# A first mixer in float32r parts: its input projections as three products each, and the first shift's modulation made by TensorE between them

## The chip, the cores and the metric

The kernel runs on one core of a Trainium2 chip. The metric is device time in microseconds (us), the median over several runs; smaller is better. The profile comes from one further execution, whose own time stands beside it.

## The reference

Two decoder layers over 256 tokens of width 1024. What matters here is the start of the first one:

```
c_act = silu(c)
mod = c_act @ ada_w[layer] + ada_b[layer]        # 1024 -> 6 * 1024
sh_m, sc_m, g_m, sh_f, sc_f, g_f = split(mod, 6)
h = rmsnorm(x, norm_mix_w) * (1 + sc_m) + sh_m
p = h @ e_w_in                                   # 1024 -> 1536: u (512), v (512), pool part (512)
ya = mixer_a(p[:, :1024])                        # gelu; layernorm of v; causal W_s in chunks of 128; u * sv
yb = mixer_b(p[:, 1024:])                        # trailing means minus the token, a 128x128 product per group
x = x + g_m * (concat(ya, yb) @ e_w_out)
```

A dense SwiGLU follows in layer 0; layer 1 has a convolution and latent attention, then a top-2-of-8 expert SwiGLU with 352 MB of weights. All inputs are float32.

## The kernel before

**Weights.** Every weight comes from HBM in chunks of 128 x 2048 float32 (1 MB) into a ring of five buffers (`raw`, line 98). The list `order` gives the sequence of the loads, all on SyncE's queue; a load is issued when the buffer five places earlier has been read for the last time. In the first stretch the sequence is, for each of four quarters q of the inner dimension: the scale's modulation chunk `("ada", 0, 1, q)`, the shift's `("ada", 0, 0, q)`, and the weight chunk `("vp", q)`; then `("u", 0)`, four chunks of the gate's modulation `("ada", 0, 2, q)` with `("u", 1)` among them, and the output projection's `("eo", c)`.

**Float32 products, and products in parts.** Most of the kernel multiplies in float32r parts: ScalarE casts a chunk to float32r (`H`, line 121, two halves), VectorE subtracts that from the chunk (`L`, line 124, two halves), the activations are split alike (lines 301 and 306, or `store_hl`), and TensorE adds H·H, L·H and H·L (`mm3_b`, lines 316, 318 and 322; `mm3_a`, lines 334, 335 and 337). Two places use plain float32 products: the v and pool columns of the first projection (line 649, a 128x512 product of each half weight with each half of the tokens) and its u columns (`gate_u`, line 666). Their operand `h0` is one float32 tile, `hF`.

**Modulation.** `ada` makes 256 of the modulation's values with two VectorE instructions of 128x1024 (line 568: multiply by silu(c), sum along the row) and an addition of the bias (line 596). `ada_rows` does the same on TensorE from weights stored by input rows: 8 products with the chunk (line 579), a copy of the result by ScalarE (line 585); the function `turn` that it gives back then turns the row into columns by two small products (line 589) and adds the bias on VectorE (line 591). Before the change `ada_rows` serves the second norm's scale and shift alone, in their last two quarters.

**Norm and transposes.** `HT.flip` transposes the normed tokens on TensorE (line 285); `HT.evac` multiplies by the scale and adds the shift from PSUM (line 299; the scale's column from line 207) and, where it splits, casts to `H` (line 301); `HT.low` makes `L` (line 306).

**Order of the work.** Between `tc.manual_schedule` and `hand.close()` the engines take their instructions as the code is written. After `hand.close()` a scheduler sets the order up to the next such stretch, in the middle of the output projection. Every engine works through its own list in order. After the vp products come `gate_u(0)`, the pooling products (lines 704 to 706, 713), `gate_u(1)`, the layernorm of v (statistics on VectorE, lines 683 to 687; the rest on GpSimd, lines 688 to 691), the product of v with `wsT` (line 730), `yaT` (lines 737 and 739), and the output projection with its residual (lines 365 and 366).

Of the kernel before, what the change touches and what calls it, by code (L numbers as in the profile page):

```python
# [17 lines left out]
D = 1024  # L18
S = 256
KD = 8  # L20
# [4 lines left out]
CH = 2048  # L25
RING = 5
RING2, RING3 = 8, 3
HB, LB = 6, 5
# [15 lines left out]
def trunk_kernel(ctx, tc, x_in, c_in, pos_in, cols_in, rows_in,  # L44
# [3 lines left out]
    vec, act, pe, gp, sp = nc.vector, nc.scalar, nc.tensor, nc.gpsimd, nc.sync  # L48
# [77 lines left out]
    def high_part(raw, f):  # L126
        h = Halves("H", HB, f)
        for q in range(2):
            h.copy(q, raw)
        return h  # L130
# [20 lines left out]
    def psa(n="pa"):  # L151
        return psA.tile([128, 512], F32, tag="A", name=nm(n))
# [16 lines left out]
    for i in range(2):  # L169
        t = per.tile([128, D], F32, name=f"x{i}")  # L170
# [137 lines left out]
    def mm3_b(outs, ks, xH, xL, wH, wL, first, last, by_tile=False):  # L308


        tiles = list(enumerate(outs))
        for group in ([[t] for t in tiles] if by_tile else [tiles]):
            for m, k in enumerate(ks):
                for i, os_ in group:
                    for n, o in enumerate(os_):
                        pe.matmul(o, xH(k, i), wH(k, n), start=first and m == 0, stop=False)  # L316
                    for n, o in enumerate(os_):
                        pe.matmul(o, xL(k, i), wH(k, n), start=False, stop=False)  # L318
            for m, k in enumerate(ks):
                for i, os_ in group:  # L320
                    for n, o in enumerate(os_):
                        pe.matmul(o, xH(k, i), wL(k, n), start=False, stop=last and m == len(ks) - 1)  # L322

    def toks(t):
        return lambda k, i: t[:, k, i * 128:(i + 1) * 128]

    def wcols(w, k0, kw, bounds):

        return lambda k, n: w[:, (k - k0) * kw + bounds[n][0]:(k - k0) * kw + bounds[n][1]]

    def mm3_a(o, wH, wL, hH, hL):

        for k in range(KD):
            pe.matmul(o, wH(k), hH[:, k, :], start=(k == 0), stop=False)  # L334
            pe.matmul(o, wH(k), hL[:, k, :], start=False, stop=False)  # L335
        for k in range(KD):
            pe.matmul(o, wL(k), hH[:, k, :], start=False, stop=(k == KD - 1))  # L337
# [210 lines left out]
    def raw_of(*key):  # L548
        fetch(place[key] + RING)
        return raws.pop(key)  # L550

    def split_of(*key):
        return split_raw(*raw_of(*key))

    def ada(l, p, q):

        half, end = ada_steps(l, p, q)
        half(0)
        half(1)
        end()  # L560
# [11 lines left out]
    def ada_rows(l, p, q, *before):  # L572

        raw, _ = raw_of("ada", l, p, q)
        ps = psb()
        for kk in range(2):
            for g in range(4):
                k = g * 2 + kk
                pe.matmul(ps[g * 32:(g + 1) * 32, 0:256], ccol[:, k:k + 1].to_broadcast([128, 32]),
                          raw[:, k * 256:(k + 1) * 256], start=(kk == 0), stop=(kk == 1), skip_group_check=True)  # L580
        j = p * 8 + q * 2
        for f in before:
            f()
        row = adp.tile([128, 512], F32, tag="junk", name=nm("row"))[:, 0:256]
        act.copy(row, ps[:, 0:256])

        def turn():
            for a in range(2):
                pe.matmul(ps[:, 256 + a:257 + a], row[:, a * 128:(a + 1) * 128], quart, start=True, stop=True)
            lo = K_AB + l * 48 + j  # L590
            vec.tensor_tensor(mods[:, l, j:j + 2], ps[:, 256:258], cols[:, lo:lo + 2], OP.add)
        return turn
# [4 lines left out]

    BD = [(0, 512), (512, 1024)]

    with Phase("mix0", w8=5, w4=5, w2=6) as pool:  # L600
        sm = pool
        lrow = pool.tile([128, 2048], F32, tag="w8", name="lrow")
        bands = pool.tile([128, 4, 3, 128], F32, tag="w8", name="bands")
# [27 lines left out]
        hand = ctx.enter_context(ExitStack())  # L631
        hand.enter_context(tc.manual_schedule(engines=MAN | {mybir.EngineType.Pool}))
        xn = normed()
        ht = HT(pool, xn, 0, False, split_it=False)
        h0 = ht.full
        vp = [[psa() for _ in range(2)] for _ in range(2)]
        ht.flip(0)
        for q in range(4):
            if q < 3:
                ht.flip(q + 1)  # L640
            ada(0, 1, q)
            ada(0, 0, q)
            ht.evac(q)
            w, _ = raw_of("vp", q)
            for kk in range(2):
                k = q * 2 + kk
                for part in range(2):
                    for i in range(2):
                        pe.matmul(vp[part][i], h0[:, k, i * 128:(i + 1) * 128],  # L649
                                  w[:, kk * D + part * 512:kk * D + (part + 1) * 512], start=(k == 0), stop=(k == 7))  # L650
            if q == 1:
                mean_bands()
        hand.close()
# [4 lines left out]
        uT = pool.tile([128, 4, S], F32, tag="w4", name="uT")  # L658

        def gate_u(c):  # L660
            w, _ = raw_of("u", c)
            ps = psb()
            for cc in range(2):
                for k in range(KD):
                    o = k * 256 + cc * 128
                    pe.matmul(ps[:, cc * 256:(cc + 1) * 256], w[:, o:o + 128], h0[:, k, :], start=(k == 0), stop=(k == 7))
            return ps

        gu_ps = gate_u(0)
# [1165 lines left out]
```

## Time and profile before

| | |
|---|---|
| median of 3 runs | 1250.69 us (1250.29 to 1253.85) |
| profiled execution: time, span | 1250.61 us, 1248.6 us |
| TensorE busy | 1199.2 us, 96% of the span |
| ScalarE, VectorE, GpSimd busy | 501.3, 735.3, 67.7 us |
| moved by DMA | 468.11 MB, mean 375 GB/s |
| granted TensorE clock, mean | 0.989 |

The profile's rows give the start and the length of an instruction or of a group in microseconds from the start of the span; PE is TensorE, PEld its weight loads, ACT ScalarE, DVE VectorE, POOL GpSimd, SP SyncE. A float32 product stands as two products in the trace (x16 for 8 instructions of line 649), a float32r product as one. In groups of pipelined products the spacing (length over count) is what one costs; the mean length of a single one includes its tail.

### The profile page before, as it was taken

The numbers are of one execution on the slowest core, as the hardware profiler recorded it, in microseconds if no ns is written. First come the engines' busy times: TensorE is split into PE (matmuls) and PEld (weight loads), VectorE is DVE, ScalarE is ACT, GpSimd is POOL, SyncE is SP. The second block draws the span as 40 slices with busy tenths as digits, with TensorE's granted clock in tenths as the row PEclk, the third lists the DMA queues.
The fourth block names the chain that finished last, engine by engine and source line by source line (L and its number), as shares of the span: only waits on it lengthen the run. The fifth ranks groups of instructions, "written<-read, shape, count | busy, mean of one in ns | idle before, by whom it ended". The sixth has DMA issues, their size and how long they took to land.

```text
span 1248.6 us, 18665 instructions
## 1 busy us (share of the span) xinstructions
PE 1199.2 (96%) x7255; PEld 866.1 (69%) x7255; DVE 735.3 (59%) x1098; ACT 501.3 (40%) x775; POOL 67.7 (5%) x105
## 2 busy tenths in 40 slices
PE   5999999999999899999999999999999999999997
PEld 2577999997987666666666676666675666666663
DVE  5797988886895355546264656263555652653531
ACT  2147443445763234444153344252433541433410
POOL 2810000001320000000000000000000000000000
PEclk9999999999999799999999999999999999999999
DMA  9898999984657899999999999999999999999995
GB/s 357 352 376 306 354 337 349 355 313 176 237 203 277 343 405 421 419 419 419 419 420 419 419 420 419 420 419 420 419 419 412 418 419 420 420 420 418 420 418 202
DMA packets 65904, 468.11 MB, mean 375 GB/s; under 512 B 7568, under 2 KB 7824, under 8 KB 9616
## 3 DMA queue, kind: packets, MB, share of 16 engines
q1 hardware_dynamic: 65520, 466.32, 92.5%
q8 instruction: 59, 0.97, 0.3%
q10 hardware_dynamic: 288, 0.52, 0.1%
q14 instruction: 37, 0.30, 0.1%
HBM read 465.76 MB, written 1.05 MB: 374 GB/s over the span
## 4 chain that ended last, share of the span: by engine, by line
PE 85%; DVE 7%; issue 2%; ACT 2%; POOL 1%; DMA 1%; SPq 0%; DVEq 0%; ACTq 0%; POOLq 0%
PE gu L1527 20%; PE o L1547 10%; PE o L316 3%; PE g L316 3%; PE pb L337 3%; PE g L318 3%; PE u L318 3%; PE o L318 3%; PE u L316 3%; PE o L322 3%; PE g L322 3%; PE pb L335 3%; PE u L322 3%; PE pb L334 3%; PE pa L649 2%
## 5 line engine op out<-in xcount | busy, mean ns | idle before, releaser
L121 ACT CAST H<-raw 128x1024 fp32r<-128x1024 f32 x350 | 344.2, 1047 | 34.2 <-PE pb L335 13.2
L147 DVE TENSOR_TENSOR raw<-raw,H 128x1024 fp32r<-128x1024 f32 x252 | 297.5, 1222 | 39.9 <-ACT H L121 22.6
L1527 PE MATMUL gu<-raw,hgS 128*64 128x256 f32 x2240 | 253.8, 383 | 0.0
L1527 PEld LDWEIGHTS gu<-raw,hgS 128*64 128x64 f32 x2240 | 157.4, 137 | 89.0 <-issue 13.8
L124 DVE TENSOR_TENSOR L<-raw,H 128x1024 fp32r<-128x1024 f32 (+1 forms) x98 | 118.2, 1219 | 26.6 <-PE pb L337 14.5
L1547 PE MATMUL o<-raw,aS 128*64 128x512 f32 x560 | 130.4, 599 | 0.0
L568 DVE SCALAR_TENSOR_TENSOR junk<-raw,cact 128x1024 bf16<-128x1024 f32 x88 | 108.8, 1259 | 8.4 <-DMA raw<-in_ada 8.2
L334 PE MATMUL pb<-hH,H 128*128 128x256 f32 x432 | 103.1, 279 | 0.0
L335 PE MATMUL pb<-hL,H 128*128 128x256 f32 x432 | 102.9, 279 | 0.0
L1533 DVE TENSOR_TENSOR msg<-msg,gu 128x256 f32<-128x256 f32 x35 | 14.7, 421 | 125.2 <-ACT msg L1532 125.1
L1547 PEld LDWEIGHTS o<-raw,aS 128*64 128x64 f32 x560 | 37.0, 137 | 64.3 <-issue 60.0
L334 PEld LDWEIGHTS pb<-hH,H 128*128 128x128 f32 x432 | 81.2, 188 | 0.4
L335 PEld LDWEIGHTS pb<-hL,H 128*128 128x128 f32 x432 | 81.1, 188 | 0.4
L1481 DVE TENSOR_TENSOR msg<-msg,u 128x512 f32<-128x512 f32 x21 | 14.4, 687 | 109.0 <-ACT msg L1480 109.0
L1532 ACT ACTIVATE msg<-gu 128x256 f32<-128x256 f32 x35 | 13.4, 384 | 161.3 <-PE gu L1527 161.2
L1480 ACT ACTIVATE msg<-g 128x512 f32<-128x512 f32 x21 | 12.5, 597 | 151.3 <-PE g L322 151.3
L316 PE MATMUL g<-H,hgH 128*128 128x512 f32 x168 | 67.3, 401 | 0.0
L322 PE MATMUL u<-raw,hgH 128*128 128x512 f32 x168 | 66.5, 396 | 0.0
L318 PE MATMUL g<-H,hgL 128*128 128x512 f32 x168 | 66.5, 396 | 0.0
L318 PE MATMUL u<-H,hgL 128*128 128x512 f32 x168 | 66.4, 395 | 0.0
L316 PE MATMUL u<-H,hgH 128*128 128x512 f32 x168 | 66.3, 395 | 0.0
L322 PE MATMUL g<-raw,hgH 128*128 128x512 f32 x168 | 66.3, 394 | 0.0
(391 smaller groups left out, 1631.4 us busy)
## 6 DMA issues: line engine op xcount, KB each, us to landing
raw<-in_mgu SPq DMA_DIRECT2D x224, 1024.0 KB, 16.0
raw<-in_mdn SPq DMA_DIRECT2D x112, 1024.0 KB, 15.3
raw<-in_ada SPq DMA_DIRECT2D x48, 1024.0 KB, 6.9
raw<-in_fgu SPq DMA_DIRECT2D x22, 1024.0 KB, 7.7
raw<-in_fdn SPq DMA_DIRECT2D x11, 1024.0 KB, 7.5
raw<-in_oin_c SPq DMA_DIRECT2D x6, 1024.0 KB, 5.3
raw<-in_ein_vp SPq DMA_DIRECT2D x4, 1024.0 KB, 9.3
raw<-in_eout SPq DMA_DIRECT2D x4, 1024.0 KB, 7.2
```

The lines of the kernel that those rows point to most:

```text
L121: act.copy(self.to(q), raw[:, q * self.f:(q + 1) * self.f])
L124: eng.tensor_tensor(self.to(q), raw[:, q * self.f:(q + 1) * self.f], high.half(q).bitcast(F32), OP.subtract)
L147: vec.tensor_tensor(l[:, at], raw[:, at], h.half(q).bitcast(F32), OP.subtract)
L316: pe.matmul(o, xH(k, i), wH(k, n), start=first and m == 0, stop=False)
L318: pe.matmul(o, xL(k, i), wH(k, n), start=False, stop=False)
L322: pe.matmul(o, xH(k, i), wL(k, n), start=False, stop=last and m == len(ks) - 1)
L334: pe.matmul(o, wH(k), hH[:, k, :], start=(k == 0), stop=False)
L335: pe.matmul(o, wH(k), hL[:, k, :], start=False, stop=False)
L337: pe.matmul(o, wL(k), hH[:, k, :], start=False, stop=(k == KD - 1))
L568: vec.scalar_tensor_tensor(junk, raw[:, a * D:(a + 1) * D], 1.0, cact, OP.mult, OP.mult, accum_out=mods[:, l, j + a:j + a + 1])
L1527: pe.matmul(gu[HALF[h], n * 256:(n + 1) * 256], g_.full[:, k, :], w[:, lo:lo + 256], start=(k == 0 and n == 0), stop=(k == KD - 1), skip_g ...
L1547: pe.matmul(o[HALF[h]], a[:, kk, c, :], w[:, kk * D + h * 512:kk * D + (h + 1) * 512], start=(j == 0 and c == 0 and kk == 0), stop=(j == 6 ...
```

## The change

The vp and u products of the first mixer become three products of float32r parts. `HT` now splits its result (`hH`, `hL` instead of `hF`). Each vp chunk is cast and subtracted in halves, and its 8 float32 products become 24 float32r products of the same size in two calls of `vp_part`, one for each 128 rows of the quarter; each u chunk is split too, and its 16 float32 products of 128x256 become 48. The shift's chunks `("ada", 0, 0, q)` leave VectorE: they are stored by input rows and go through `ada_rows`, the products with chunk q + 1 between the two calls of `vp_part` of quarter q, and `turn` at the head of quarter q + 1. One more 8 KB buffer is given to the phase. The sequence of the loads is as before.

```diff
         xn = normed()
-        ht = HT(pool, xn, 0, False, split_it=False)
-        h0 = ht.full
+        ht = HT(pool, xn, 0, False)
+        h0H, h0L = ht.H, ht.L
         vp = [[psa() for _ in range(2)] for _ in range(2)]
+
+        def vp_part(q, ks, w):
+            mm3_b([[vp[part][i] for part in range(2)] for i in range(2)], ks, toks(h0H), toks(h0L),
+                  wcols(w[0], q * 2, D, BD), wcols(w[1], q * 2, D, BD), ks[0] == 0, ks[-1] == KD - 1)
+
         ht.flip(0)
+        ada(0, 1, 0)
+        turn = ada_rows(0, 0, 0)
         for q in range(4):
+            turn()
+            ht.evac(q)
+            raw, _ = raw_of("vp", q)
+            w = high_part(raw, CH), Halves("L", LB, CH)
+            ht.low(q, vec)
+            for half in range(2):
+                w[1].less(half, raw, w[0])
             if q < 3:
                 ht.flip(q + 1)
-            ada(0, 1, q)
-            ada(0, 0, q)
-            ht.evac(q)
-            w, _ = raw_of("vp", q)
-            for kk in range(2):
-                k = q * 2 + kk
-                for part in range(2):
-                    for i in range(2):
-                        pe.matmul(vp[part][i], h0[:, k, i * 128:(i + 1) * 128],
-                                  w[:, kk * D + part * 512:kk * D + (part + 1) * 512], start=(k == 0), stop=(k == 7))
+                ada(0, 1, q + 1)
+            vp_part(q, (q * 2,), w)
+            if q < 3:
+                turn = ada_rows(0, 0, q + 1)
+            vp_part(q, (q * 2 + 1,), w)
             if q == 1:
                 mean_bands()
         hand.close()
...
         def gate_u(c):
-            w, _ = raw_of("u", c)
+            w = split_of("u", c)
             ps = psb()
             for cc in range(2):
-                for k in range(KD):
-                    o = k * 256 + cc * 128
-                    pe.matmul(ps[:, cc * 256:(cc + 1) * 256], w[:, o:o + 128], h0[:, k, :], start=(k == 0), stop=(k == 7))
+                mm3_a(ps[:, cc * 256:(cc + 1) * 256], *(lambda k, t=t: t[:, k * 256 + cc * 128:k * 256 + cc * 128 + 128] for t in w),
+                      h0H, h0L)
             return ps
```

TensorE's list, before, from the end of the vp quarter 0 into quarter 1 (`pt` is the transposes' PSUM tile, `pa` the four sums of vp, `raw` the weight chunk, `hF` the activations):

```order
L649 MATMUL pa_156<-raw_172,hF_153 128x512
L649 MATMUL pa_157<-raw_172,hF_153 128x512
L285 MATMUL pt_204<-ident,xn_137 128x128 x2
L285 MATMUL pt_204<-ident,xn_138 128x128 x2
L649 MATMUL pa_154<-raw_183,hF_153 128x512
L649 MATMUL pa_155<-raw_183,hF_153 128x512
```

Between two quarters TensorE has only the transposes of the quarter after next. The same place now (`pb_238` holds the shift's row of quarter 1 and, after line 589, its columns; `H_272` is the first half of the vp chunk of quarter 1):

```order
L322 MATMUL pa_155<-L_210,hH_153 128x512
L322 MATMUL pa_157<-L_210,hH_153 128x512
L322 MATMUL pa_156<-L_210,hH_153 128x512
L322 MATMUL pa_158<-L_210,hH_153 128x512
L589 MATMUL pb_238<-quart,row_247 128x1 x2
L285 MATMUL pt_281<-ident,xn_137 128x128 x2
L285 MATMUL pt_281<-ident,xn_138 128x128 x2
L316 MATMUL pa_155<-H_272,hH_153 128x512
L316 MATMUL pa_157<-H_272,hH_153 128x512
```

The turning products of quarter 1's shift now stand behind the last product of quarter 0. ScalarE's list, before, after the norm (`v` and `pp` are vp's results):

```order
L261 ACTIVATE xn_137<-x_92,ss_135 128x1024
L261 ACTIVATE xn_138<-x_94,ss_136 128x1024
L673 ACT_TABLE_LOAD
L673 ACTIVATE v_367<-pa_154 128x512
L673 ACTIVATE v_369<-pa_155 128x512
```

The same list now, from quarter 0 into quarter 1 (`hf` is what `evac` wrote):

```order
L301 CAST hH_153<-hf_197 128x512
L121 CAST H_203<-raw_168 128x1024
L121 CAST H_205<-raw_168 128x1024
L585 COPY row_247<-pb_238 128x256
L301 CAST hH_153<-hf_266 128x512
L121 CAST H_272<-raw_179 128x1024
L121 CAST H_274<-raw_179 128x1024
```

ScalarE had nothing to do between norm and results; now a quarter's weight casts stand behind the cast of its activations. VectorE's list, before, from the last `evac` on (`bn`, `mv`, `lrs` are the layernorm's statistics):

```order
L299 TENSOR_SCALAR hF_153<-pt_265,acol_315,mods 128x256 x2
L683 BN_STATS bn_376<-v_367 128x6
L683 BN_STATS bn_386<-v_369 128x6
L685 BN_AGGR mv_378<-bn_376 128x2
L685 BN_AGGR mv_388<-bn_386 128x2
L687 TENSOR_SCALAR lrs_380<-mv_378 128x1
L687 TENSOR_SCALAR lrs_390<-mv_388 128x1
```

The same stretch now, from the last half of vp's low part on (`raw_369` is the first u chunk, 405 and 439 are chunks of the gate's modulation):

```order
L124 TENSOR_TENSOR L_448<-raw_307,H_443 128x1024
L568 SCALAR_TENSOR_TENSOR junk_481,mods<-raw_405,cact 128x1024
L568 SCALAR_TENSOR_TENSOR junk_483,mods<-raw_405,cact 128x1024
L124 TENSOR_TENSOR L_499<-raw_369,H_495 128x1024
L596 TENSOR_TENSOR mods<-mods,cols 128x2
L568 SCALAR_TENSOR_TENSOR junk_488,mods<-raw_439,cact 128x1024
L568 SCALAR_TENSOR_TENSOR junk_490,mods<-raw_439,cact 128x1024
L124 TENSOR_TENSOR L_501<-raw_369,H_497 128x1024
L596 TENSOR_TENSOR mods<-mods,cols 128x2
L691 BN_STATS bn_561<-v_552 128x6
L691 BN_STATS bn_571<-v_554 128x6
L693 BN_AGGR mv_563<-bn_561 128x2
```

The scheduler put four modulation instructions and both low halves of the first u chunk ahead of the layernorm's statistics.

## Rows read from the trace of the kernel before

**Rows 1.** The page's first line.

```profile
span 1248.6 us, 18665 instructions
```

**Rows 2.** Windows: stretch, length, each engine's busy time (instructions), clock, DMA share, GB/s.

```profile
17.00:52.00 35.00, 32.19 (x74) 14.46 (x75) 22.14 (x47) 1.98 (x4) 20.31 (x28) 1.00 0.97 388
52.00:71.00 19.00, 19.00 (x104) 16.87 (x103) 15.55 (x23) 5.99 (x12) 14.47 (x8) 1.00 0.81 320
71.00:82.00 11.00, 11.00 (x57) 9.14 (x57) 10.93 (x16) 8.28 (x11) 0.00 (x0) 1.00 0.91 359
115.00:260.00 145.00, 145.00 (x1055) 136.35 (x1054) 128.80 (x217) 66.46 (x92) 0.00 (x0) 1.00 0.92 343
500.00:1240.00 740.00, 729.66 (x4275) 479.40 (x4276) 367.45 (x417) 279.55 (x369) 0.00 (x0) 1.00 1.00 413
```

**Rows 3.** Timeline of TensorE, the vp products: start, length, idle before.

```profile
17.04 9.94 PE L649 MATMUL pa<-raw,hF 128*128 128x512 f32 x16 [3.49 <-DVE hF L299]
...
44.62 7.13 PE L649 MATMUL pa<-raw,hF 128*128 128x512 f32 x16 [1.09 <-DVE hF L299]
```

**Rows 4.** Chain that ended last, 0 to 140 us: start, length, work.

```profile
51.76 6.91 PE pb L666 x32
...
70.06 0.91 PE pt L730 x8
70.98 0.70 DVE yaT L737
```

**Rows 5.** The same chain, float32r products in parts.

```profile
117.26 0.96 PE pb L337 x8
...
135.36 0.47 PE pa L318 x2
```

**Rows 6.** Timeline, single steps of the kind that the change adds or moves.

```profile
13.70 1.22 DVE L568 SCALAR_TENSOR_TENSOR junk<-raw,cact 128x1024 bf16<-128x1024 f32 x1
...
16.45 0.99 DVE L299 TENSOR_SCALAR hF<-pt,acol,mods 128x256 f32<-128x256 f32 x2
...
50.71 0.69 DVE L683 BATCH_NORM_STATS2 bn<-v 128x6 f32<-128x512 f32 x1 [0.16 <-ACT v L673]
...
81.22 2.36 DVE L124 TENSOR_TENSOR L<-raw,H 128x1024 fp32r<-128x1024 f32 x2
...
98.42 1.07 PE L579 MATMUL pb<-raw,ccol 128*32 128x256 f32 x16
...
99.25 0.69 DVE L366 TENSOR_TENSOR x<-x,res 128x512 f32<-128x512 f32 x1
99.56 0.60 PE L589 MATMUL pb<-quart,row 128*128 128x1 f32 x4
...
100.28 0.16 DVE L591 TENSOR_TENSOR mods<-pb,cols 128x2 f32<-128x2 f32 x1 [0.33 <-PE pb L589]
100.47 0.16 DVE L207 SCALAR_TENSOR_TENSOR acol<-mods,cols 128x2 f32<-128x2 f32 x1
...
110.09 0.61 ACT L301 CAST hH<-hf 128x512 fp32r<-128x512 f32 x1
110.61 1.04 ACT L121 CAST H<-raw 128x1024 fp32r<-128x1024 f32 x1
```

**Rows 7.** Timeline of GpSimd's layernorm of v, and VectorE beside it.

```profile
51.75 1.61 POOL L688 TENSOR_TENSOR lrs<-lrs,nhalf 128x1 f32<-128x1 f32 x1 [3.00 <-DVE lrs L687]
...
58.27 2.28 DVE L568 SCALAR_TENSOR_TENSOR junk<-raw,cact 128x1024 bf16<-128x1024 f32 x1
...
63.71 1.27 POOL L690 TENSOR_TENSOR v<-v,lrow 128x512 f32<-128x512 f32 x1
65.06 1.60 POOL L691 TENSOR_TENSOR v<-v,lrow 128x512 f32<-128x512 f32 x1
```

**Rows 8.** Windows around the one early stretch of lower clock.

```profile
107.00:109.00 2.00, 1.37 (x8) 1.34 (x8) 1.92 (x5) 1.92 (x4) 0.00 (x0) 0.76 1.04 434
109.00:111.40 2.40, 2.40 (x14) 2.40 (x13) 1.62 (x4) 2.40 (x4) 0.00 (x0) 0.50 0.80 331
```

More of the change, by code (lines that the diff above doesn't have):

```diff
@@ L598, in trunk_kernel @@
     BD = [(0, 512), (512, 1024)]
-    with Phase("mix0", w8=5, w4=5, w2=6) as pool:
+    with Phase("mix0", w8=6, w4=5, w2=6) as pool:
         sm = pool
@@ L1806 @@
     by_d = I["ada_w"][0].reshape(8, 128, 6, 4, 256).transpose(2, 3, 1, 0, 4).reshape(6, 4, 128, 2, 1024)
-    ada[0, 3:5, 2:4] = by_d[3:5, 2:4]
+    ada[0, 3:5, 2:4], ada[0, 0] = by_d[3:5, 2:4], by_d[0]
     arrays = {
```

## The prediction

> **What bounds the kernel now.** I read the page's span first, then the windows by stage, then the chain that ended last, and for single durations the timeline. The span is 1248.6 us in an execution of 1250.61 us [rows 1], so 2.0 us lie around it; the median of the three runs is 0.08 us above that execution, which is nothing here. From 115 us on a delay cannot be made up: TensorE is busy 145.00 of 145.00 us in the dense SwiGLU, and the experts' stretch has a DMA share of 1.00 [rows 2]. The code there is unchanged and its loads come through a ring of five, so what the first mixer loses or gains arrives at the end whole. Only the first 100 us decide.
>
> In them three things take turns. From 17 to 52 us the vp products run in four bursts, the last two with pauses ahead that end on VectorE (1.09 us at 44.62) [rows 3]. They end, and the u products begin, at 51.76 us [rows 4]: burst 0 ended at 17.04 + 9.94 = 26.98, so a later quarter takes (51.76 - 26.98) / 3 = 8.26 us. From 52 to 71 us TensorE is never idle (19.00 of 19.00) [rows 2]; `yaT` starts at 70.98 behind line 730 [rows 4]. From there VectorE is the chain (10.93 of 11.00 us in the next stretch) [rows 2], and its last residual ends at 99.25 + 0.69 = 99.94 us [rows 6].
>
> **What goes and comes, by engine.** Off VectorE go eight modulation instructions at 1.22 us, 9.8 us. On it come twelve low halves of weights at 1.18 (2.36 a pair) and four low parts of activations, about 0.69 each by a two-operand instruction of their size: 14.2 + 2.8 = 17.0 us [rows 6]. VectorE has 7 us more. On TensorE a quarter's 7.13 us become 24 products at 0.47 / 2, 5.6 us [rows 3, 5]; a u chunk's 6.91 become 48 at 0.96 / 8, 5.8 us [rows 4, 5]; but four `ada_rows` at 1.07 and four turns at 0.60 come on [rows 6]. That is -6.1 - 2.2 + 6.7 = -1.6 us. So the sums promise next to nothing, and the order of the lists decides.
>
> **1. The first product.** The first shift chunk has landed by 13.70, when VectorE went on to it without a wait [rows 6]. TensorE's 8 products for it take 1.07 us at full clock; at the start it isn't at full clock, since the first vp burst took 9.94 us instead of 7.13 [rows 3], so about 2.1. The copy and the turn follow: from the first product to line 591 the row shows 98.42 to 100.28, 1.86 us, and 1.07 more at half clock, which gives 16.6 to 16.9. Then line 207 (0.19 after line 591), `evac` 0.16 later for 0.99, the cast of 0.61, and ScalarE's first weight half of 1.04 [rows 6]: 19.9 us against 17.04.
>
> **2. The first quarter.** If full clock comes when it came before (about 22.9 us, where a burst that lost 2.8 us must have changed), 6.4 of 24 products run at 0.47, the rest at 0.235, and `ada_rows` of the next quarter adds 1.07: 28.0 us against 26.98, so +1.0.
>
> **3. Three more quarters.** In front of each stands a serial chain, by the lists as they now stand: turn to line 591 (99.56 to 100.28, 0.72), line 207 0.19, `evac` after 0.16 for 0.99, cast 0.61, then the weight's first half 1.04, because ScalarE's list has it behind that cast however early the chunk landed. That is 3.7 us [rows 6] in which TensorE has nothing but turn and transposes. With 5.6 of products and 1.07 of `ada_rows` a quarter takes 10.4 us, the last 9.3: 28.0 + 30.1 = 58.1 us against 51.76, +6.3. VectorE's low halves (1.18 each) end before the eight high products are through and don't count. Nor does the ring: the vp chunk is now released by VectorE rather than by TensorE's last product, so SP's loads go out earlier, never later.
>
> **4. From vp to `yaT`.** TensorE's work here is 2.2 us shorter, but VectorE's list decides. Its vp low halves end at 58.1 - 5.6 + 2.4 = 54.9. Then come two modulation instructions, a u low half, two more, the other u half: six at 1.18 (a modulation instruction taken back to back as long as a low half), 62.0. The layernorm's statistics began 0.6 before 50.71 and handed over to GpSimd at 51.75 [rows 6, 7], 1.65 us, and one more modulation instruction now stands among them: 64.8. GpSimd's eight instructions took 51.75 to 66.66, 14.9 us, hidden under TensorE's 19 us; now nothing hides them. Bounds: eight at the shortest, 1.27, give 10.2 us, and the row gives 14.9 [rows 7]. VectorE works beside them for some 8 us (seven such instructions) instead of throughout, so I take 13, nearer to the row. With half of line 730's 0.91 us `yaT` starts at 78.3, +7.3; by the bounds +4.5 to +9.2.
>
> On VectorE and GpSimd side by side the trace shows a modulation instruction of 2.28 us instead of 1.22 while GpSimd works [rows 7]. The Trainium skill, "SBUF — State Buffer", section "Who interferes with whom", says that the two share a port pair and that a two-input VectorE instruction and a reading GpSimd one exclude each other for a whole instruction. The row agrees. Taken to the end it speaks against this change, which puts more two-input instructions on VectorE there; that is the third rival.
>
> **5. From `yaT` to the residual.** Before, one low half of the output projection lay ahead of `yaT`; now VectorE's list has three there. Two fewer are left, -2.4 us, on a stretch where VectorE is the chain. So +4.9 at the residual, with ends +2.1 and +6.8.
>
> **6. The clock.** In the only early stretch where the granted clock falls it reads 0.76 and then 0.50 of full (1.2 of 2.4 GHz), about 0.96 + 2.40 = 3.4 us at half, after TensorE had been in use 1.37 of 2 us in short pieces [rows 8]. Half of that, 1.7 us, is lost. The change makes three pauses of 3.7 us in the vp stage and may raise the clock later at the start, by up to the 2.9 us that the first product is late, 1.45 us. None to all of these: 0 to 6.5; I take one, 1.5. The Trainium skill, "TensorE: Matmul & The Clock Gate", section "HAM oscillation — how this bites in real kernels", says that pauses between bursts of products throw the clock back. The pauses before, 1.09 us long [rows 3], show no fall; whether 3.7 us do, no row shows. By that rule all three would, rival two.
>
> **Sum.** 4.9 + 1.5 = +6.4 us, against 1250.61: **1257.0 us**.
>
> **Rivals.**
> - *The pauses are covered, faster.* For it: the pauses before waited for data, the ring is now freed earlier, and the products themselves are shorter. If TensorE went from quarter to quarter without a pause, a quarter would take 6.7 instead of 8.26, the last 5.6: +1.0 - 1.6 - 1.6 - 2.7 = -4.9; then 2.2 less in u and 2.4 less after `yaT`: -9.5, 1241 us. It decides from a pause of 1.6 us downwards (8.26 - 6.7). Against it: every link of the 3.7 us is in an in-order list behind the one before.
> - *The clock falls in every pause, and rises late.* 4.9 + 6.5 = +11.4, 1262 us. For it the lower clock after broken use [rows 8], against it the bursts of 5.6 us between.
> - *VectorE and GpSimd exclude each other.* Eight GpSimd instructions at 1.27 that each wait for one VectorE instruction of 1.18 take 19.6 us: `yaT` at 84.9, +13.9 - 2.4 + 1.5 = +13.0, 1263.6 us. Against it: VectorE runs out of work after 8 us, and the row before is 14.9.
> - *GpSimd at its shortest, the clock as before.* +2.1, 1252.7 us: no change that can be told.
>
> **How the numbers follow.** My forecast 0.54, the clock 0.13, the exclusion 0.06, GpSimd short 0.18, pauses covered 0.09. About 0.3%, 3.75 us, is what this measurement can tell from no change: within 1246.9 to 1254.4 lies only the fourth rival. So faster 0.09, same 0.18, slower 0.73. The range leaves out the faster case and the far end of the slow ones: 1251.5 to 1262.5 us.
>
> **What would show it.** In the changed profile: the first float32r product of vp near 20 us; four bursts with idle time ahead of the last three that ends on ScalarE's weight half (line 121), 3 to 4 us from the last product of a quarter to the first of the next; u products from about 58 us; line 696, the first layernorm step on GpSimd, near 65 us; TensorE waiting for GpSimd ahead of line 738; the last residual near 105 us; from then on the same lengths. I am wrong if u begins before 52 us, or if `yaT` starts before 72 us in spite of a late vp, or if the dense stage takes back what was lost.

## The result and the profile after

The changed kernel takes 1264.91 us (median of six runs, 1260.21 to 1267.98) against 1251.10 (1250.29 to 1253.85) for the kernel before, run in turn with it on one chip: a ratio of 1.0104, 95% interval 1.0089 to 1.0119. It is slower, as forecast, but by 13.8 us where 6.4 were forecast, and it lies outside the range of 1251.5 to 1262.5. The profiled execution took 1265.51 us. Its six runs lie 7.8 us apart, those of the kernel before 3.6.

The page's first line and the windows that answer to [rows 1, 2]; the columns are the same, the stretches are moved to where the stages now lie:

```profile
span 1263.7 us, 18990 instructions
```
```profile
17.00:65.00 48.00, 37.16 (x168) 27.28 (x167) 31.32 (x52) 14.80 (x19) 17.96 (x27) 0.86 0.83 321
65.00:87.00 22.00, 17.57 (x138) 16.81 (x137) 16.63 (x25) 12.22 (x20) 15.51 (x8) 0.98 0.84 335
87.00:98.00 11.00, 11.00 (x52) 9.17 (x52) 9.95 (x16) 6.00 (x8) 0.00 (x0) 0.88 0.31 103
130.00:275.00 145.00, 145.00 (x1055) 136.36 (x1054) 128.69 (x218) 66.62 (x92) 0.00 (x0) 1.00 0.92 345
500.00:1240.00 740.00, 731.38 (x4261) 483.35 (x4261) 371.99 (x419) 282.74 (x372) 0.00 (x0) 1.00 1.01 419
```

The dense stage and the experts' stage read as before (TensorE 145.00 of 145.00 us with 1055 products, a DMA share of 1.01). The loss is whole in the first 115 us: the vp stage is 48 us long instead of 35, its granted clock is 0.86 instead of 1.00, and the stretch to `yaT` is 22 us instead of 19, with TensorE idle for 4.4 of them.

TensorE's timeline of the changed kernel from the end of the first quarter answers to [rows 3, 4]:

```profile
28.93 0.50 PE L589 MATMUL pb<-quart,row 128*128 128x1 f32 x4
29.30 0.63 PE L285 MATMUL pt<-ident,xn 128*128 128x128 f32 x4
32.65 1.22 PE L316 MATMUL pa<-H,hH 128*128 128x512 f32 x2 [2.71 <-ACT H L121]
33.66 1.06 PE L318 MATMUL pa<-H,hL 128*128 128x512 f32 x2
...
39.75 0.63 PE L318 MATMUL pa<-H,hL 128*128 128x512 f32 x2
...
45.73 1.22 PE L316 MATMUL pa<-H,hH 128*128 128x512 f32 x2 [2.65 <-ACT H L121]
...
57.81 0.73 PE L316 MATMUL pa<-H,hH 128*128 128x512 f32 x2 [3.41 <-ACT H L121]
...
65.04 0.28 PE L334 MATMUL pb<-hH,H 128*128 128x256 f32 x1
```

Each pause runs from the turn (line 589) to the first product of the next quarter and ends on ScalarE's first weight half (line 121). A pair of products of one kind (line 318) takes 1.06 us behind the first pause and 0.63 a few us later. The windows of the same kernel show why: 0.50 is the lower of the clock's two levels, 1.2 of 2.4 GHz.

```profile
32.00:38.00 6.00, 5.36 (x12) 3.84 (x12) 5.71 (x8) 1.54 (x2) 5.69 (x5) 0.50 0.86 321
39.00:45.00 6.00, 4.07 (x28) 3.12 (x20) 1.60 (x5) 1.26 (x3) 4.82 (x10) 1.00 0.98 358
45.50:48.50 3.00, 2.77 (x7) 2.20 (x8) 2.79 (x3) 1.12 (x2) 0.60 (x1) 0.50 0.43 157
59.00:62.00 3.00, 3.00 (x9) 2.35 (x8) 3.00 (x5) 2.89 (x3) 0.00 (x0) 0.50 0.20 38
86.00:89.50 3.50, 3.50 (x16) 3.23 (x16) 2.29 (x4) 0.00 (x0) 0.00 (x0) 0.52 0.10 37
```

GpSimd's layernorm of v and TensorE's wait for it answer to [rows 7] and to line 730 of [rows 4]:

```profile
69.69 1.54 POOL L696 TENSOR_TENSOR lrs<-lrs,nhalf 128x1 f32<-128x1 f32 x1 [20.48 <-DVE mv L693]
71.34 3.67 POOL L697 TENSOR_SCALAR v<-v,mv,lrs 128x512 f32<-128x512 f32 x1
75.10 1.96 POOL L698 TENSOR_TENSOR v<-v,lrow 128x512 f32<-128x512 f32 x1
77.14 2.22 POOL L699 TENSOR_TENSOR v<-v,lrow 128x512 f32<-128x512 f32 x1
...
80.98 2.08 POOL L697 TENSOR_SCALAR v<-v,mv,lrs 128x512 f32<-128x512 f32 x1
...
84.49 1.26 POOL L699 TENSOR_TENSOR v<-v,lrow 128x512 f32<-128x512 f32 x1
...
85.80 3.08 PE L738 MATMUL pt<-wsT,v 128*128 128x128 f32 x14 [4.27 <-POOL v L699]
...
87.21 0.69 DVE L745 TENSOR_TENSOR yaT<-pt,lrow 128x512 f32<-128x512 f32 x1 [4.09 <-PE pt L738]
```

Eight instructions last from 69.69 to 85.75, 16.06 us. Line 699 takes 2.22 us while VectorE runs low halves and 1.26 us at the end, where VectorE waits for `yaT` (4.09 us idle).

### The profile page after: what moved, and what is told of

It reads as the page before. It is cut to its first block, busy times and chain, and to the rows that moved or that the text cites. A ratio compares the mean times of both kernels' runs of the same rounds, so it can differ in the third digit from the quotient of the medians.

```text
span 1263.7 us, 18990 instructions
## 1 busy us (share of the span) xinstructions
PE 1206.0 (95%) x7399; PEld 880.4 (70%) x7399; DVE 740.7 (59%) x1098; ACT 515.6 (41%) x795; POOL 66.3 (5%) x105
## 3 DMA queue, kind: packets, MB, share of 16 engines
HBM read 465.76 MB, written 1.05 MB: 369 GB/s over the span
## 4 chain that ended last, share of the span: by engine, by line
PE 84%; DVE 8%; ACT 3%; POOL 2%; DMA 1%; issue 1%; SPq 0%; DVEq 0%; ACTq 0%; POOLq 0%
PE gu L1535 20%; PE o L1555 10%; PE o L316 3%; PE g L316 3%; PE pb L337 3%; PE g L318 3%; PE u L318 3%; PE o L318 3%; PE o L322 3%; PE u L316 3%; PE g L322 3%; PE pb L335 3%; PE u L322 3%; PE pb L334 3%; PE pa L316 2%; PE pa L318 2%
## 5 line engine op out<-in xcount | busy, mean ns | idle before, releaser
L121 ACT CAST H<-raw 128x1024 fp32r<-128x1024 f32 x362 | 355.9, 1047 | 27.9 <-PE pb L335 9.9
L147 DVE TENSOR_TENSOR raw<-raw,H 128x1024 fp32r<-128x1024 f32 x252 | 297.5, 1222 | 39.6 <-ACT H L121 22.2
L124 DVE TENSOR_TENSOR L<-raw,H 128x1024 fp32r<-128x1024 f32 (+1 forms) x110 | 133.3, 1227 | 29.7 <-PE pb L337 14.9
L334 PE MATMUL pb<-hH,H 128*128 128x256 f32 x464 | 110.8, 279 | 0.0
L335 PE MATMUL pb<-hL,H 128*128 128x256 f32 x464 | 110.5, 279 | 0.0
L568 DVE SCALAR_TENSOR_TENSOR junk<-raw,cact 128x1024 bf16<-128x1024 f32 x80 | 98.0, 1244 | 1.0 <-DMA raw<-in_ada 0.9
L334 PEld LDWEIGHTS pb<-hH,H 128*128 128x128 f32 x464 | 87.2, 188 | 0.5
L335 PEld LDWEIGHTS pb<-hL,H 128*128 128x128 f32 x464 | 87.1, 188 | 0.4
```

The lines of the kernel that those rows point to most:

```text
L121: act.copy(self.to(q), raw[:, q * self.f:(q + 1) * self.f])
L124: eng.tensor_tensor(self.to(q), raw[:, q * self.f:(q + 1) * self.f], high.half(q).bitcast(F32), OP.subtract)
L147: vec.tensor_tensor(l[:, at], raw[:, at], h.half(q).bitcast(F32), OP.subtract)
L568: vec.scalar_tensor_tensor(junk, raw[:, a * D:(a + 1) * D], 1.0, cact, OP.mult, OP.mult, accum_out=mods[:, l, j + a:j + a + 1])
```

## The experiments

Two theories stood at the start. The clock: TensorE's granted clock falls in the vp pauses and costs about 5 us. The chain on GpSimd: v's layernorm, late and exposed, costs some 3 us more than forecast. Against both: the float32r parts themselves (casts, low halves, VectorE's longer list) are the cost wherever they stand. Each ratio is against the kernel before, measured beside it (median 1250.66 to 1251.92 us). In the code cuts, `...` stands for lines left out.

**Filled pauses.**

```diff
                 ada(0, 1, q + 1)
+            for _ in range(6 if q else 2):
+                pe.matmul(turn.ps[:, 0:256], ident, xn[0][:, 0:256], start=True, stop=True, ...)
             vp_part(q, (q * 2,), w)
```

> The changed kernel, with filler products of TensorE in the pause of each vp quarter, between the turns and the first weight half: two in quarter 0, six in each of the other three, 128x256 float32 products whose results nobody reads. Nothing else is changed. Theory C (the clock): TensorE's idle pauses of 3.7 us are what the granted clock falls after, and the falls cost vp about 5 us (first product of the fourth quarter at 57.75 instead of 52.5). With the pauses filled the granted clock stays full in vp, the fourth quarter's first product starts at 52.5 to 54, vp ends near 60, the time is 1259 to 1261 us and the five times scatter less than the 7 us of the changed kernel. Rival (the chain turn, eviction, cast, weight cast and the split work itself are the whole cost, the clock only follows): vp's end moves under 1 us and the time stays 1264 to 1267 us.

Measured 1261.35 us (1260.17 to 1262.47), ratio 1.0077 [1.0063, 1.0090]. The timeline (the fillers are line 658) and the window of vp with the fillers in place:

```profile
26.80 0.50 PE L589 MATMUL pb<-quart,row 128*128 128x1 f32 x4
...
27.63 2.85 PE L658 MATMUL pb<-xn,ident 128*128 128x256 f32 x12
30.31 0.73 PE L316 MATMUL pa<-H,hH 128*128 128x512 f32 x2
...
57.77 0.28 PE L334 MATMUL pb<-hH,H 128*128 128x256 f32 x1
...
63.97 1.54 POOL L699 TENSOR_TENSOR lrs<-lrs,nhalf 128x1 f32<-128x1 f32 x1 [14.58 <-DVE mv L696]
```
```profile
17.00:58.00 41.00, 39.68 (x207) 29.73 (x207) 29.45 (x48) 15.10 (x20) 22.05 (x27) 1.00 0.91 367
```

The clock stays at 1.00 and u begins at 57.77, 7.3 us earlier, with pauses about as long as they were (26.80 to 30.31). Not all of the 7.3 us is the falls. 0.6 us is a first product that came earlier (19.23 instead of 19.85; the first transposes, ahead of any filler, are as much earlier), 1.5 us was won in the first quarter, where the products reached full clock sooner, and 5.1 us in the three quarters behind it (26.80 to 57.77, 30.97 us, instead of 28.93 to 65.04, 36.11 us). With the pauses filled no fall is left in vp, so the falls come from the pauses; they cost vp 5.1 us, as theory C said.

The end gained less. The median is 3.6 us lower, the two intervals just touch, and 1261.35 lies a little above theory C's 1261. GpSimd starts at 63.97 here, 6.2 us behind vp's end instead of 4.65, and its chain takes 16.5 us, so `yaT` is 5.0 us earlier, at 82.22. The five runs lie 2.3 us apart; the kernel before spreads by 2.9 to 5.3 us in its four measurements, so this says little about scatter.

**Half of GpSimd's chain on VectorE.**

```diff
-            gp.tensor_scalar(v, v, mv[:, 0:1], r, ...)     # and the two lines behind it
+            on = vec if i else gp
+            on.tensor_scalar(v, v, mv[:, 0:1], r, ...)
```

> The changed kernel, with the layernorm of the second token half of v (subtract and scale, weight, bias: three instructions) on VectorE instead of GpSimd. Theory G: GpSimd's chain after vp (69.69 to 85.75, 16.06 us, with TensorE waiting 4.3 us at its end for v) stands on the path. Halved, the last v comes 4 to 6 us earlier, TensorE's wait for v goes, yaT starts 4 to 5 us earlier than 87.21, and the time is 1259.5 to 1261.5 us. Rival (VectorE is what bounds this stretch, its list only grows by three instructions of 0.6 to 0.8 us): yaT starts at 86 to 88 and the time is 1264 to 1267 us.

Measured 1263.85 us, ratio 1.0096 [1.0080, 1.0112]: no difference from the changed kernel. Two rows of VectorE and TensorE show where the gain went:

```profile
78.37 0.55 DVE L698 TENSOR_SCALAR v<-v,mv,lrs 128x512 f32<-128x512 f32 x1 [5.25 <-POOL lrs L696]
...
80.17 0.87 PE L337 MATMUL pb<-hH,L 128*128 128x256 f32 x4 [3.20 <-DVE L L124]
```

VectorE stood 5.25 us behind the second inverse root, which GpSimd makes after the first half's chain; u's low half stood behind that, and TensorE waited 3.20 us for it. One wait was traded for another. Both theory G's time and its earlier `yaT` were missed.

**u in plain float32.**

```diff
-            w = split_of("u", c)
+            w, _ = raw_of("u", c)
...          # plain products with h0 as in the kernel before
```

> The changed kernel with the u product put back to plain float32 (no casts and no low halves of the u weights; the activations are kept in float32 beside their parts, and for their room three small scratch buffers fewer). vp stays three products. What of the cost is u's: by the prediction's step 4, two low halves of 0.96 us stand ahead of the statistics on VectorE, so GpSimd's chain starts 2 us earlier than 69.69, and u's own products take longer behind cover: time 1261.5 to 1264 us, vp's end unchanged at 65. Rival (u as three products pays for itself, TensorE is what bounds between vp's end and yaT): the time is 1265 to 1270 us. If the time falls below 1260 us the u part was the larger half of the loss, against both.

Measured 1262.23 us, ratio 1.0085 [1.0069, 1.0101], inside the range expected, though the interval overlaps that of the changed kernel. "vp's end unchanged" missed: u needs no low halves, so 3.70 us of it fill the pause ahead of the last quarter, and vp ends at 60.7. The profiled execution also has one fall in vp and not three. Behind its first pause, 3.52 us from turn to product (28.74 to 32.26) against 3.72, there is none:

```profile
32.26 0.73 PE L317 MATMUL pa<-H,hH 128*128 128x512 f32 x2 [2.52 <-ACT H L121]
32.83 0.63 PE L319 MATMUL pa<-H,hL 128*128 128x512 f32 x2
```

**The shift back on VectorE, vp and u as three products.**

```diff
-        turn = ada_rows(0, 0, 0)
+        ada(0, 0, 0)
...
-            turn()
...
                 ada(0, 1, q + 1)
+                ada(0, 0, q + 1)
             vp_part(q, (q * 2,), w)
-            if q < 3:
-                turn = ada_rows(0, 0, q + 1)
```

> The changed kernel with the shift's modulation chunks back on VectorE, in the layout and order of the kernel before (each quarter's shift right behind its scale); vp and u stay three products. Tells the two halves of the change apart. Theory S (the serial chain turn, eviction, cast, first weight half on TensorE is what made each quarter longer): TensorE's pauses of 3.7 us go, a quarter takes what VectorE's list takes, 9 to 9.5 us, vp ends near 53 to 56, time 1252 to 1257 us. Rival (the three products with their casts and low halves cost it, wherever the shift is made): vp ends at 62 or later and the time is 1262 us or more.

Measured 1262.84 us, ratio 1.0088 [1.0075, 1.0101]. vp ends at 56.63, 8.4 us earlier, but its pauses are there without any turn (TensorE's timeline, and VectorE's eviction ahead of the first of them):

```profile
28.58 1.12 PE L316 MATMUL pa<-H,hH 128*128 128x512 f32 x2 [2.37 <-ACT H L121]
...
39.77 1.22 PE L316 MATMUL pa<-H,hH 128*128 128x512 f32 x2 [3.35 <-ACT H L121]
```
```profile
24.20 1.22 DVE L568 SCALAR_TENSOR_TENSOR junk<-raw,cact 128x1024 bf16<-128x1024 f32 x1
...
25.93 1.00 DVE L299 TENSOR_SCALAR hf<-pt,acol,mods 128x256 f32<-128x256 f32 x2
```

What makes these pauses is VectorE's list. It is busy without a break from the low halves of one quarter (18.29) through the modulation instructions to the eviction of the next (25.93), and from there to the first product the cast and the weight half follow as before. So a quarter takes what VectorE's list takes, as theory S said, but 10.3 to 11.2 us (eviction to eviction: 15.66, 25.93, 37.11, 48.09) where it said 9 to 9.5. The clock falls here too (0.87 in vp). GpSimd starts 6.8 us behind vp's end and takes 16.5. vp's end lies near theory S's 53 to 56, the time at the rival's 1262. The profiled execution (1258.96) is the fastest of the five, so what the median loses beyond it isn't in this trace.

**The shift on TensorE alone, vp and u in plain float32.** The edit as against the changed kernel, beside the turn and the row products that stay:

```diff
-            vp_part(q, (q * 2,), w)
+            vp_half(0)          # pe.matmul(vp[part][i], h0[...], w[...]), plain float32
...
-            w = split_of("u", c)
+            w, _ = raw_of("u", c)
```

> The other half of the change alone: vp and u in plain float32 as before, the first shift's modulation chunks by TensorE as in the changed kernel (row products between the two halves of a quarter, turn at the head of the next). Theory S (each turn starts a serial chain on TensorE's path): the pause at each quarter's head is turn, addition, scale, eviction, some 2.5 us against 1.1 to 1.7 before, a quarter is 7.1 + 1.5 + 2.5 = 11 us instead of 8.2 to 9.2, vp ends near 56 to 58 and the time is 1254 to 1258 us. Rival (VectorE, relieved of 2.6 us per quarter, was what bounded before, and the short turn is hidden): vp ends at 51 to 53 and the time is 1249 to 1252 us.

Measured 1260.03 us (1253.87 to 1262.31), ratio 1.0080 [1.0067, 1.0094]. The pauses of 2.5 us aren't there: from the turn to the first product pass 1.57 and 1.64 us, 0.57 and 0.64 of them idle. The row products and turns themselves take 1.57 us a quarter, vp ends 4.4 us later than before (56.03 against 51.59, 1.4 of it products of u that stand ahead), and a wait for a chunk comes on. The chunk is the last quarter's shift; SyncE issues its load behind that of the vp chunk, where the kernel before issues it ahead:

```profile
37.82 3.70 PE L650 MATMUL pa<-raw,hF 128*128 128x512 f32 x8 [0.64 <-DVE hF L299]
42.88 1.07 PE L580 MATMUL pb<-raw,ccol 128*32 128x256 f32 x16 [1.36 <-DMA raw<-in_ada]
```
```profile
31.11 0.33 SPq L98 DMA_DIRECT2D raw<-in_ein_vp  x1
36.37 0.33 SPq L98 DMA_DIRECT2D raw<-in_ada  x1
```

So this wait may belong to the sequence of the loads, which this kernel changes too (it asks for one or two chunks fewer ahead while a vp chunk is in use), and not to the products; that was not tested. The profiled execution (1253.87) is the fastest of the five and shows no fall of the clock in the mixer; where the other four lose 4 to 8 us more isn't seen in it.

**The turn early.**

```diff
+        w = prepare(0)      # weight casts, turn, evac, low halves, flip and scale of the next
         for q in range(4):
+            if q < 3:
+                turn = ada_rows(0, 0, q + 1)
             vp_part(q, (q * 2,), w)
+            now = w
+            if q < 3:
+                w = prepare(q + 1)
-            vp_part(q, (q * 2 + 1,), w)
+            vp_part(q, (q * 2 + 1,), now)
```

> The changed kernel with the same work in another order in vp: the row products of quarter q+1 stand before quarter q's first weight half, its turn, eviction and casts between q's two halves, so that TensorE has 2.9 us of products beside the chain, and the casts of the next weights stand ahead of the activation's on ScalarE. Theory P (the order of the chain, with the clock's falls in its pauses, is the whole loss in vp; the parts themselves cost nothing there): pauses under 1 us, granted clock full from 25 on in vp, a quarter takes 8 to 9 us, vp ends at 52 to 55 instead of 65; what follows keeps its length (22 us to yaT), so 1253 to 1257 us. Rival (weights arrive at one chunk of 1 MB per 2.6 us and three chunks make a quarter of 8 us, or VectorE's list of 7.5 to 9 us bounds): quarters of 10 us or more, vp's end at 58 or later, 1259 us or more.

Measured 1257.59 us (1255.79 to 1259.33), ratio 1.0058 [1.0045, 1.0071]. The window of vp, and what TensorE waits for in it and behind it:

```profile
17.00:54.00 37.00, 32.01 (x174) 24.01 (x173) 29.43 (x47) 13.51 (x18) 22.53 (x27) 1.00 0.99 398
```
```profile
40.73 1.07 PE L579 MATMUL pb<-raw,ccol 128*32 128x256 f32 x16 [1.27 <-DMA raw<-in_ada]
...
77.73 1.65 PE L746 MATMUL pt<-wsT,v 128*128 128x128 f32 x6 [7.66 <-POOL v L707]
```

The pauses and falls are gone, vp ends at 54.3, 10.8 us earlier, and what TensorE now waits for in vp is the weights, with a DMA share of 0.99. That is a floor which the kernel before nearly stood on: three chunks of 1.05 MB a quarter at 388 GB/s [rows 2] are 8.1 us, and its quarters took 8.26. The gain stops at 7.3 us because TensorE then waits 7.66 us for GpSimd's v. In vp theory P came true, apart from waits for chunks above its 1 us; "what follows keeps its length" did not: `yaT` starts 25.1 us behind vp's end (79.42), not 22, and the time is just above its 1257.

**v's statistics first on VectorE.** Only the order of VectorE's list behind vp is changed.

```diff
         hand.close()
-        ada(0, 2, 0)
-        ada(0, 2, 1)
+        hand2.enter_context(tc.manual_schedule(engines={mybir.EngineType.DVE}))
...
             vec.tensor_scalar(r, mv[:, 1:2], EPS, None, op0=OP.add)   # both halves, then GpSimd's chain
...
+        ada(0, 2, 0)
+        ada(0, 2, 1)
+        hand2.close()
```

> The changed kernel with one order changed on VectorE behind vp: v's statistics stand right behind u's first two low halves, and the scale's next modulation chunks behind them; GpSimd's work is the same. Theory G (GpSimd's chain from the statistics to the last v is on the path): GpSimd starts 2 to 2.5 us behind vp's end instead of 4.65, the last v and yaT come 2 us earlier or more, time 1261 to 1263 us. Rival (the chain only gets slower beside VectorE's two-operand instructions, or the second u's low halves come late instead): yaT as late as before, 1264 to 1266 us.

Measured 1262.19 us, ratio 1.0097 [1.0081, 1.0114]: no difference that can be told from the changed kernel. GpSimd starts earlier behind vp's end (62.94 to 64.26, 1.3 us) and still takes 16.7 us, and u's second low half comes late (TensorE waits 1.78 us for it). The median lies in theory G's range, but not by its mechanism: `yaT` is 1.7 us earlier, at 85.52, because vp ended 2.1 us earlier in this execution; from vp's end it takes 22.6 us against 22.2. The rival holds.

**Turn early, statistics first, half of v on VectorE**, with both inverse roots first on GpSimd. On top of the turn-early edit:

```diff
+        for mv, r in rs:
+            gp.tensor_tensor(r, r, nhalf[:, 0:1], OP.pow)
+        for i in range(2):
+            (mv, r), v, on = rs[i], vs[i], (gp, vec)[i]
+            if i:
+                ada(0, 2, 0)
+            on.tensor_scalar(v, v, mv[:, 0:1], r, op0=OP.subtract, op1=OP.mult)
```

> The order of the turn-early kernel in vp, v's statistics first on VectorE, and the second token half of v's layernorm on VectorE with both inverse roots taken first on GpSimd. Both theories together (vp's serial chain, then GpSimd's chain, and nothing else): vp ends at 52 to 55, the last v is ready 10 us later, before TensorE is through u and the pooled products (16 us), so yaT at 69 to 73, about where it stood before (70.98), and the time is 1249 to 1253 us: no change against the kernel before, or a little faster. Rival (the split work itself on VectorE and ScalarE, or the weights' arrival, bounds this stretch): 1256 us or more.

Measured 1255.81 us, ratio 1.0037 [1.0025, 1.0049]: 9.1 us better than the changed kernel, still 4.9 slower than the kernel before (1250.96 beside it), and between the two ranges. vp ends at 54.9, but `yaT` comes at 77.31 instead of 69 to 73. v is ready at 64.6 and line 754 runs at 66.00 without a wait; what is late is u's low half:

```profile
69.12 1.22 DVE L124 TENSOR_TENSOR L<-raw,H 128x1024 fp32r<-128x1024 f32 x1
...
70.40 0.74 PE L337 MATMUL pb<-hH,L 128*128 128x256 f32 x4 [2.45 <-DVE L L124]
```
```profile
55.00:77.00 22.00, 19.08 (x141) 18.39 (x140) 21.15 (x35) 11.98 (x20) 6.37 (x5) 0.92 0.75 275
77.00:100.00 23.00, 20.43 (x85) 15.97 (x84) 22.02 (x35) 6.79 (x11) 0.00 (x0) 0.93 0.82 322
```

VectorE (the third busy time) is at 21.15 of 22 and 22.02 of 23 us: now it bounds.

**The same with u's second low halves moved ahead**, and **the same with u in plain float32**: two ways to ask whether it is VectorE's order or its sum. The edits to the kernel just shown:

```diff
+        wu1 = split_of("u", 1)          # the first: ahead of ada(0, 2, 1)
-        gu_ps = gate_u(1)
+        gu_ps = gate_u(1, wu1)
...
-            w = split_of("u", c)        # the second
+            w, _ = raw_of("u", c)
```

> The same best order with u as three products, and the second u chunk's casts and low halves ahead of the scale's second and third modulation chunk on VectorE. Theory V (VectorE's list bounds as a whole): what is gained at u's products (2.9 us of waiting) comes back at the output product's low halves, 1254 to 1256.5 us. Rival (only the order of the list was wrong): TensorE has no wait over 0.5 us between vp's end and the residual, 1251.5 to 1253.5 us.

> The best order so far (turn early in vp, statistics first, second token half of v on VectorE) with u in plain float32: four low halves of 1.22 us fewer on VectorE, 3 us more of products on TensorE. Theory V (with both chains mended, VectorE's list from 50 to 100, busy 9.2 to 10 of each 10 us, is what is left of the loss): no wait of TensorE for u's low halves (2.45 and 0.47 us), no clock fall behind it, residual 3 to 4 us earlier, time 1252 to 1254 us. Rival (TensorE and the weights' arrival bound behind vp, VectorE only follows): the 3 us of products show, 1256 to 1259 us.

The first measured 1255.72 us, ratio 1.0037 [1.0025, 1.0050], the same as without the move: the wait comes back at the output product, 2.28 us for a low half at 91.66. The second measured 1253.10 us (1251.02 to 1254.77, 12 runs), ratio 1.0018 [1.0007, 1.0028]. So the sum it is; u as three products costs 2.6 us in this order (1255.72 less 1253.10, measured together). TensorE's timeline in the kernel with u plain:

```profile
114.42 0.74 PE L865 MATMUL pb<-hH,L 128*128 128x256 f32 x4 [0.16 <-DVE L L124]
```
The mixer ends almost as before: this product of the dense stage comes at 114.42 here and its like at 113.75 in the kernel before. The profiled execution (1251.02) is the fastest of the twelve. What the median loses beyond it isn't in this trace and stays open; from 115 to 500 us the granted clock reads 0.98 on the mean here and in the kernel before.

**The order mended, the shift alone on TensorE, vp and u plain.** The edit is that of v's statistics and layernorm above, made to the kernel with vp and u in plain float32; its main lines:

```diff
+        for mv, r in rs:
             gp.tensor_tensor(r, r, nhalf[:, 0:1], OP.pow)
...
+            (mv, r), v, on = rs[i], vs[i], (gp, vec)[i]
```

> The kernel with vp and u in plain float32 and the shift's chunks by TensorE, with the same mended order behind vp (statistics first on VectorE, both inverse roots first on GpSimd, second token half of v on VectorE). Theory G: what that half of the change costs alone is GpSimd's late chain (it started at 59.83 against 51.75) more than vp's end (3 us later): mended, yaT comes at 72 to 74 instead of 78 and the time is 1251.5 to 1255 us. Rival (the row products on TensorE, 1.6 us a quarter with vp's quarters already at 8.6 us, are the loss): 1257 to 1260 us, as without the mend.

Measured 1259.04 us, ratio 1.0062 [1.0043, 1.0080]. Theory G falls here: v is ready in time, `yaT` still comes at 79.31, because vp ends 8 us later than in the kernel before (59.9 against 51.6, 1.4 of it products of u that stand ahead), with a wait of 2.19 us for the shift's chunk and the clock at 0.61 behind it:

```profile
45.10 1.43 PE L580 MATMUL pb<-raw,ccol 128*32 128x256 f32 x16 [2.19 <-DMA raw<-in_ada]
```
```profile
45.00:48.00 3.00, 2.90 (x18) 1.33 (x19) 0.00 (x0) 1.36 (x2) 0.00 (x0) 0.61 1.03 404
```

The code of vp is that of the kernel with the shift alone on TensorE, whose profiled execution, its fastest, ended vp at 56.03 without a fall. So this is one place where its slower executions may lose their time; the load of the chunk goes out late here too (37.94, the vp chunk's at 32.64).

No version tried beats the kernel before.

## Why the prediction was right in direction and wrong in size

By its own steps, in the profiled execution (+15.1 us of span):

1. **First product**: 19.85 for 19.9. Right.
2. **First quarter**: it ended at 28.93 for 28.0. The products run at half clock until about 24.7 (line 322 at 23.43 takes 1.67 us for four, line 579 at 25.03 the full-clock 1.07), not 22.9: full clock came 1.8 us later, where the first product came 2.8 us later. +0.9.
3. **Three quarters**: the pauses are 3.72, 3.65 and 3.91 us for 3.7, link by link as listed. TensorE's share of a quarter is what failed: the three took 13.15, 11.82 and 11.14 us for 10.4, 10.4 and 9.3, 6.0 us more, because products behind each pause ran at half clock (5.1 of the 6.0 by the fillers). u began at 65.04 for 58.1, 6.9 late. With the clock held by the fillers the three took 30.97 us for 30.1 and u began at 57.77: the step was right for a steady clock. "Earlier, never later" was wrong of the loads (the last vp chunk's went out at 37.74 instead of 34.74, since the quarters were late), but TensorE waited for none of them in vp.
4. **vp to `yaT`**: GpSimd started 4.65 us behind vp's end for 6.7 (-2.05); its chain took 16.06 for 13, above the upper bound of 14.9 (+3.06); behind it TensorE's line 738 ran at half clock (+0.96). Together +2.0. Taking less than the row of before, since VectorE would be busy beside it for only part of the time, was the mistake: VectorE had two-input instructions beside the whole first half.
5. **`yaT` to the residual**: 28.05 us (87.21 to 115.26) for 26.6. A step of -0.9 instead of -2.4, the stretch partly at half clock (0.88 in 87 to 98). +1.5.
6. **The clock**: one fall of 1.5 us was taken. The trace shows four falls in the mixer and a late rise; the rise (0.9) and the three falls in vp (5.1, which is three times the 1.7 that the step had for one) make 6.0 us. This is the step that failed: the term was mis-sized, and its own upper bound, 6.5 us, was the better value.

0.9 + 6.0 (step 3) + 2.0 + 1.5 = 10.4 more at the residual than the +4.9 that stood there, so +15.3, and +15.1 at the end; the 1.5 of step 6 came on top in the forecast. The direction was right by the mechanism forecast, the pauses of 3.7 us and GpSimd's exposed chain, and not by luck. Of the rivals, "the clock falls in every pause" was the mechanism, and it had 0.13; it gave 1262 us because it left GpSimd at 13. Against it I had set "the bursts of 5.6 us between", which did not hold the clock up. The Trainium skill, "TensorE: Matmul & The Clock Gate", section "HAM oscillation — how this bites in real kernels", says that pauses between bursts throw the clock back. The filled pauses agree: 1.00 with them, 0.86 without. How much a pause brings differs: behind the first one the changed kernel runs at half clock from its first pair of products on (1.22 us at 32.65), the statistics-first kernel has the pair at 31.51 in 0.73 and only a later one in 1.06, and the kernel with u plain none at half clock there at all (0.63 at 32.83).

"VectorE and GpSimd exclude each other" gave 19.6 us for the chain and 16.06 were measured. The Trainium skill, "SBUF — State Buffer", section "Who interferes with whom", makes the shared ports an exclusive lock. The trace agrees in part. Both engines pay (line 699 took 2.22 us beside VectorE's low halves and 1.26 alone, a modulation instruction beside line 697 1.63 instead of 1.22), and VectorE's short addition of line 596, mostly 0.16 us, took 1.12 at 75.96 and ended with GpSimd's line 698. But not every pair excludes each other: line 697 took its shortest time, 2.08 us at 80.98, while a low half beside it took its usual 1.22 at 81.89.

What the prediction did not name at all is the floor. At the rate of [rows 2] vp's weights arrive in 8.1 us a quarter and the quarters took 8.26, so shorter products had next to nothing to win there, while every stall comes on top. The rival "pauses covered", 1241 us with quarters of 6.7 us, left this out: with the pauses covered, in the turn-early kernel, the turns stand 8.4 and 8.9 us apart (27.31, 35.67, 44.62).

What stays open: how the loss divides between the two halves of the change can't be given as a sum. Alone they cost 10.9 us (vp and u) and 9.1 us (shift, with loads in another sequence), together 13.8: both make TensorE wait in vp, and the falls that follow are shared. The falls in other executions than the profiled ones are seen only in their mean clock (0.980 to 0.988 for the changed kernel, the slower runs at the lower end).

## What to carry to other kernels

Before products are made cheaper, divide the bytes that the stage loads by the rate that its windows show: where a burst already takes that long, the gain is near zero and only the risk is left. A pause on TensorE can cost twice, once as itself and once as half clock behind it (here 11 us of pauses brought 5 us more); price both, or give TensorE something to do, best by taking the serial chain between the two halves of the burst before. And when work is moved, follow the engine that was hidden: GpSimd's 15 us had been covered by TensorE's 19, and each cure handed the wait to the next engine, GpSimd to VectorE, until its sum bounded.

## What the runs showed of the hardware that was not expected

- Products that nobody reads made the kernel faster: the fillers, 2.85 us of TensorE in each of three quarters, took 5.1 us off these quarters in the trace and 3.6 us off the median, where the two intervals just touch.
- Over the start of the kernel the granted clock reads 1.00 (20 to 24 us) while a pair of products takes 1.05 us there and 0.63 from 26 us on: the column doesn't show the first rise, the durations do:

```profile
20.00:24.00 4.00, 4.00 (x10) 3.13 (x11) 4.00 (x5) 0.74 (x1) 0.00 (x0) 1.00 1.01 422
```
```profile
20.87 1.05 PE L318 MATMUL pa<-H,hL 128*128 128x512 f32 x2
...
26.61 0.63 PE L318 MATMUL pa<-H,hL 128*128 128x512 f32 x2
```

- One GpSimd instruction, the subtract and scale of v, took from 2.08 us (at 61.49 in the kernel with the shift alone on TensorE, VectorE idle beside it) to 4.09 us (at 72.52 in the statistics-first kernel, beside VectorE's modulation instructions), with operands of the same shape.
